# A float32 layer on one core: wide matmuls for the high weight tiles of the up-projection, and another order of the last norm and its stores

## The chip, the core and the metric

The kernel runs on one core of one Trainium2 chip. A core has a matrix engine (TensorE, in the profile PE, with its weight loads as PEld), VectorE (DVE), ScalarE (ACT), GpSimd (POOL) and SyncE (SP), which here mostly issues transfers. Each engine works through its own list of instructions in order and waits on semaphores of the others. TensorE writes its results to PSUM; this kernel's pools there hold eight tiles of up to 512 float32 columns, called banks below. The metric is device time of one execution, in microseconds; a kernel's time is the median of its runs.

## The reference, cut to what matters

One layer of a language model on 256 tokens with a width of 2048, all in float32. Two mixers (a state-space one and a gating one) read one projection of the normed input, are normed, projected back and added to `x`. The change touches only what follows:

```python
h = rmsnorm(x, norm_mlp_g[l])
x = x + jnp.square(jax.nn.relu(h @ w_up[l])) @ w_down[l]     # 2048 -> 8192 -> 2048
...
return rmsnorm(x, norm_final_g)
```

`rmsnorm` multiplies a row by the inverse root of its mean square plus 1e-6 and by a vector of gains.

## The kernel before

**Float32 in three products.** Matmuls here take operands in the format `F32R`. Each float32 operand is kept as two of these: a high part, which is a copy in that format, and a low part, the rest. A product is then three matmuls: high weight by high activation, high weight by low activation, and low weight by high activation. Weights come from memory in float32 and are split on the chip: `wparts` loads two k-steps (2 x 128 rows by 512 columns, 512 KB) into a buffer `raw` (four of them), ScalarE copies it to `whi` (L105), and VectorE subtracts to get `wlo` (L106). There are three buffers each of `whi` and `wlo`, so a split can begin only when TensorE has finished with the buffer three back.

**The two kinds of block.** `block_A` (up-projection, also part of the input projection) holds weights as the stationary operand: for each of four column tiles `m` and each k-step it runs three matmuls of 256 columns, the tokens (L186, L187, L188). Two column tiles share a bank of PSUM, so a block of 512 output features takes two banks. `block_B` (down-projection) holds activations as the stationary operand and streams 512 weight columns (L202 to L204). Both take their banks from one pool of four, `psa`; two other pools, `psx` and `pss`, hold the other four banks for the mixers and the transposes.

**The MLP.** Four rounds `f`, each with four up blocks (16 k-steps, 2048 hidden features in all) and then four down blocks that add to `dacc`. After each up block, for each of its two banks, ScalarE applies ReLU into `rl` (L1004), VectorE multiplies by the positive part, which squares it (L1005, `sqm`), ScalarE copies to the high half of `hT` (L1006) and VectorE subtracts for the low half (L1007). The row factor of the norm before the MLP is applied only at the end, squared, as `rs2q`.

**The end.** The last 512 columns of the last round are done apart: their weights are split ahead into spare memory (`wlast`), then token tile 0 runs with 512 columns and token tile 1 in two halves of 256 (L1048 to L1050, `accL`). `last_add` adds the residual, and squares with a row sum into `ss3` (L984, L987). Then VectorE adds up the row's eight sums (L1054), `rstd_sqrt` makes the inverse root (L268 to L273: a square root on ScalarE, a reciprocal and one Newton step on VectorE), the four quarters of the row tile are scaled (L1059, L1061 on VectorE, L1063 on ScalarE), and each is stored from SyncE's queue (L1064).

**What sets the order.** The order on each engine is not written out: a scheduler places the instructions by its own estimate of when each can run, within what data and buffers allow. It chooses, for example, where the copies of one up block fall between the weight splits of the next.

Of the kernel before, what the change touches and what calls it, by code (L numbers as in the profile page):

```python
# [18 lines left out]
P = 128  # L19
# [30 lines left out]
def hybrid_layer_kernel(  # L50
# [19 lines left out]
    psx = ctx.enter_context(tc.tile_pool(name="psx", bufs=1, space=PSUM))  # L70
    pss_ = ctx.enter_context(tc.tile_pool(name="pss", bufs=3, space=PSUM))
    wp1 = ctx.enter_context(tc.tile_pool(name="wp1", bufs=3))
    tmpool = ctx.enter_context(tc.tile_pool(name="tmpool", bufs=2))
    front = ExitStack()
    sp = front.enter_context(tc.tile_pool(name="ssmp", bufs=1))
# [3 lines left out]
    def nm(s):  # L79
        uid[0] += 1  # L80
        return f"{s}_{uid[0]}"
# [3 lines left out]

    def acc(shape, name="acc"):
        return psa.tile(shape, F32, tag="acc", name=nm(name))
# [103 lines left out]

    def block_B(w, k0, nk, c0, act):

        banks = [acc([P, 512], "accB") for _ in range(2)]
        for kp0, hi, lo in wparts(w, k0, nk, c0):
            for t in range(2):
                ts_ = slice(t * P, t * P + P)
                for kk in range(KS):
                    kp = kp0 + kk
                    xh, xl = act(kp)  # L200
                    with behind():
                        T.matmul(banks[t], xh[:, ts_], hi[:, kk], start=(kp == 0), stop=False)  # L202
                    T.matmul(banks[t], xh[:, ts_], lo[:, kk], start=False, stop=False)  # L203
                    T.matmul(banks[t], xl[:, ts_], hi[:, kk], start=False, stop=(kp == nk - 1))  # L204
                    pump(stream["d"] / 4)
        return banks
# [57 lines left out]
    def rstd_sqrt(dst, ss, scale, n):  # L264

        m = const.tile([P, n], F32, name=nm("rq_m"))
        t1 = const.tile([P, n], F32, name=nm("rq_t"))
        A.activation(dst, ss, AF.Sqrt, scale=scale, bias=eps_c)  # L268
        V.tensor_scalar(m, ss, scale, EPS, ALU.mult, ALU.add)
        V.reciprocal(dst, dst)  # L270
        V.tensor_tensor(t1, dst, dst, ALU.mult)
        V.scalar_tensor_tensor(t1, t1, -0.5, m, ALU.mult, ALU.mult)
        V.scalar_tensor_tensor(dst, t1, 1.5, dst, ALU.add, ALU.mult)  # L273
# [699 lines left out]
    front.close()  # L973
    mp = ctx.enter_context(tc.tile_pool(name="mlp", bufs=1))
# [6 lines left out]
    def last_add(t, c, cw, bank):  # L981
# [6 lines left out]
        if c < D - 512:  # L988
            V.tensor_tensor(d_, d_, gfin[:, c : c + cw], ALU.mult)


    def act_x2T(k):
        return x2T[:, k, 0], x2T[:, k, 1]

    NF = 4
    for f in range(NF):
        hT = []
        for cb in range(4):
            banks = block_A(w_up, 0, 16, f * 2048 + cb * 512, act_x2T)
            ht = mp.tile([P, 4, 2, S], F32R, tag="hT", bufs=6, name=nm("hT"))  # L1000
            for i in range(2):
                rl = mp.tile([P, 2, S], F32, tag="rl", bufs=2, name=nm("rl"))
                sq = mp.tile([P, 2, S], F32, tag="sqm", bufs=2, name=nm("sqm"))
                A.activation(rl, banks[i], AF.Relu)  # L1004
                V.scalar_tensor_tensor(sq, banks[i], 0.0, rl, ALU.max, ALU.mult)  # L1005
# [32 lines left out]
    for t in range(2):  # L1038
        ts_ = slice(t * P, t * P + P)
        cw = 512 if t == 0 else 256  # L1040
        for c in range(0, 512, cw):
            bank = acc([P, cw], "accL")
            for kp0, hi, lo in parts:
                for kk in range(KS):
# [5 lines left out]
                    T.matmul(bank, xl[:, ts_], wh, start=False, stop=(kp == 15))  # L1050
            last_add(t, c0 + c, cw, bank)
        s3 = const.tile([P, 1], F32, name=nm("s3"))
        r3 = const.tile([P, 1], F32, name=nm("r3"))
        V.tensor_reduce(s3, ss3[:, t], AX.X, ALU.add)  # L1054
        rstd_sqrt(r3, s3, 1.0 / D, 1)
        for n in range(4):
            ns = slice(n * 512, (n + 1) * 512)
            if n == 0:
                V.tensor_scalar(dacc[:, t, ns], dacc[:, t, ns], r3, None, ALU.mult)  # L1059
            elif n == 3:  # L1060
                V.scalar_tensor_tensor(dacc[:, t, ns], dacc[:, t, ns], r3, gfin[:, ns], ALU.mult, ALU.mult)  # L1061
            else:
                A.activation(dacc[:, t, ns], dacc[:, t, ns], AF.Copy, scale=r3)  # L1063
            nc.sync.dma_start(out[t * P : (t + 1) * P, ns], dacc[:, t, ns])  # L1064
# [29 lines left out]
```

## Time and profile before

| | |
|---|---|
| three timed runs | 1059.5, 1062.08, 1062.22 us; median 1062.08 |
| the profiled execution: time, span | 1060.78 us, 1059.0 us |
| TensorE busy | 1043.3 us (99%) |
| VectorE, ScalarE busy | 651.3 us (62%), 532.1 us (50%) |
| up blocks' matmuls, first and last start | 331.7 and 962.3 us |
| mean granted clock of TensorE | 0.994 |
| moved by DMA | 195.25 MB, 184 GB/s |

The span runs from the first to the last instruction; the execution's time has 1.78 us around it. A row of the timeline gives start, length in microseconds, engine, line and operation, the tile written and the tiles read, shapes, and in brackets how long the engine had been idle and what ended that. Names of tiles stand without their buffer numbers. The length of a matmul row contains the way through the array, and rows overlap, so the rate of a stream is read from the starts.

### The profile page before, as it was taken

What the parts mean: (1) busy time and instruction counts of PE and PEld (TensorE: products, weight loads), DVE (VectorE), ACT (ScalarE), POOL (GpSimd) and SP (SyncE); (2) the same over time, 40 slices, a digit from 0 to 9 for tenths busy, and PEclk for the clock granted to TensorE, in tenths of its full rate; (3) what the DMA queues carried; (4) which work ended last, traced back from release to release, by engine and by line L of the source; (5) the groups of instructions that cost most, each with busy time, mean ns of one, the idle gap of its engine ahead of it and who ended that gap; (6) DMA issues with size and microseconds to landing.
All of it is one profiled execution on the core that took longest, in us unless ns stands there. A gap on an engine that the chain in (4) does not pass through costs nothing.

```text
span 1059.0 us, 16980 instructions
## 1 busy us (share of the span) xinstructions
PE 1043.3 (99%) x6881; PEld 951.1 (90%) x6881; DVE 651.3 (62%) x888; ACT 532.1 (50%) x685; POOL 9.5 (1%) x22
## 2 busy tenths in 40 slices
PE   8999999999999999999999999999999999999996
PEld 7997899978989999888999988899998889998886
DVE  6899988686687555544455555545555565555564
ACT  5668676663766444544444443344444434444453
POOL 0101000000000000000000000000000000000000
PEclk8999999999999999999999999999999999999998
DMA  8774554566565666666666666666666666666662
GB/s 239 225 224 133 141 159 105 155 219 196 181 221 178 180 183 184 191 193 192 192 181 182 187 189 196 198 182 183 184 187 191 191 197 182 184 184 187 195 205 97
DMA packets 112047, 195.25 MB, mean 184 GB/s; under 512 B 17753, under 2 KB 21537, under 8 KB 111521
## 3 DMA queue, kind: packets, MB, share of 16 engines
q1 hardware_dynamic: 111712, 194.13, 61.4%
q8 instruction: 54, 0.88, 0.4%
q14 instruction: 25, 0.20, 0.1%
q0 software_dynamic: 256, 0.03, 0.0%
HBM read 189.91 MB, written 4.19 MB: 183 GB/s over the span
## 4 chain that ended last, share of the span: by engine, by line
PE 90%; ACT 3%; DVE 3%; DMA 2%; issue 1%; SPq 0%; ACTq 0%
PE accA L186 14%; PE accA L188 14%; PE accA L187 14%; PE accB L203 14%; PE accB L204 14%; PE accB L202 14%; PE pf L664 1%; DMA raw<-in_w_in_dram 1%; ACT Tp L631 1%; DMA bcn<-in_ssm_c_im_dram 1%; DVE wlo L106 1%; PE py L704 1%; PE accL L1050 1%; PE accL L1049 1%; PE accL L1048 1%
## 5 line engine op out<-in xcount | busy, mean ns | idle before, releaser
L106 DVE TENSOR_TENSOR wlo<-raw,whi 128x1024 fp32r<-128x1024 f32 (+1 forms) x337 | 411.3, 1221 | 372.1 <-ACT whi L105 371.5
L105 ACT ACTIVATE whi<-raw 128x1024 fp32r<-128x1024 f32 (+1 forms) x337 | 355.9, 1058 | 454.9 <-PE accB L204 200.9
L186 PE MATMUL accA<-x2T,whi 128*128 128x256 f32 x1024 | 289.6, 283 | 0.0
L187 PE MATMUL accA<-x2T,whi 128*128 128x256 f32 x1024 | 289.6, 283 | 0.0
L188 PE MATMUL accA<-x2T,wlo 128*128 128x256 f32 x1024 | 289.2, 283 | 0.0
L187 PEld LDWEIGHTS accA<-x2T,whi 128*128 128x128 f32 x1024 | 196.6, 192 | 0.2
L186 PEld LDWEIGHTS accA<-x2T,whi 128*128 128x128 f32 x1024 | 196.6, 192 | 0.2
L188 PEld LDWEIGHTS accA<-x2T,wlo 128*128 128x128 f32 x1024 | 196.3, 192 | 0.0
L203 PE MATMUL accB<-wlo,hT 128*128 128x512 f32 x480 | 186.8, 389 | 0.0
L204 PE MATMUL accB<-whi,hT 128*128 128x512 f32 x480 | 186.7, 389 | 0.0
L202 PE MATMUL accB<-whi,hT 128*128 128x512 f32 x480 | 168.0, 389 | 0.0
L204 PEld LDWEIGHTS accB<-whi,hT 128*128 128x128 f32 x480 | 90.1, 188 | 18.7
L203 PEld LDWEIGHTS accB<-wlo,hT 128*128 128x128 f32 x480 | 90.1, 188 | 18.5
L202 PEld LDWEIGHTS accB<-whi,hT 128*128 128x128 f32 x480 | 90.1, 188 | 18.6
L186 PE MATMUL accA<-xT,whi 128*128 128x256 f32 x256 | 73.5, 294 | 2.4 <-ACT xT L300 2.4
L187 PE MATMUL accA<-xT,whi 128*128 128x256 f32 x256 | 73.8, 291 | 0.0
L188 PE MATMUL accA<-xT,wlo 128*128 128x256 f32 x256 | 72.5, 290 | 0.0
L186 PEld LDWEIGHTS accA<-xT,whi 128*128 128x128 f32 x256 | 49.3, 195 | 3.3 <-ACT xT L300 2.7
L187 PEld LDWEIGHTS accA<-xT,whi 128*128 128x128 f32 x256 | 50.0, 195 | 0.6 <-DVE xT L301 0.3
L188 PEld LDWEIGHTS accA<-xT,wlo 128*128 128x128 f32 x256 | 49.5, 196 | 0.2
L203 PE MATMUL accB<-wlo,xT 128*128 128x512 f32 x64 | 25.8, 403 | 0.0
L204 PE MATMUL accB<-whi,xT 128*128 128x512 f32 x64 | 25.1, 392 | 0.0
(285 smaller groups left out, 1079.9 us busy)
## 6 DMA issues: line engine op xcount, KB each, us to landing
raw<-in_w_up_dram SPq DMA_DIRECT2D x128, 512.0 KB, 3.7
raw<-in_w_down_dram SPq DMA_DIRECT2D x128, 512.0 KB, 4.0
raw<-in_w_in_dram SPq DMA_DIRECT2D x47, 512.0 KB, 4.2
raw<-in_w_out_dram SPq DMA_DIRECT2D x32, 512.0 KB, 4.7
raw<-in_ssm_glu_w_dram SPq DMA_DIRECT2D x8, 512.0 KB, 4.4
x<-in_x_dram SPq DMA_DIRECT2D x2, 1024.0 KB
out_dram<-dacc SPq DMA_DIRECT2D x8, 256.0 KB, 2.6
xin<-in_x_dram SPq DMA_DIRECT2D x6, 256.0 KB, 7.1
```

Source lines behind the costliest of these rows:

```text
L105: A.activation(hi, src, AF.Copy)
L106: V.tensor_sub(lo, src, hi.bitcast(F32))
L186: T.matmul(o, hi[:, kk, ms], xh, start=first, stop=False, skip_group_check=True)
L187: T.matmul(o, hi[:, kk, ms], xl, start=False, stop=False, skip_group_check=True)
L188: T.matmul(o, lo[:, kk, ms], xh, start=False, stop=(kp == nk - 1), skip_group_check=True)
L202: T.matmul(banks[t], xh[:, ts_], hi[:, kk], start=(kp == 0), stop=False)
L203: T.matmul(banks[t], xh[:, ts_], lo[:, kk], start=False, stop=False)
L204: T.matmul(banks[t], xl[:, ts_], hi[:, kk], start=False, stop=(kp == nk - 1))
L631: A.activation(Tp[e * 32 : (e + 1) * 32, :, g, 3 - e : 4, :], k4[:, :, 0 : e + 1, :], AF.Copy, scale=gmask[:, g : g + 1],)
L664: T.matmul(pfs[r][i][:, q], w1s[r][:, i, q], u2[r][:, q], start=True, stop=True)
L704: last = T.matmul(py[g * 64 : (g + 1) * 64, q], Gp[:, q, g].rearrange("p j c -> p (j c)"), Eg[:, q, g], start=False, stop=True, skip_group ...
L1048: T.matmul(bank, xh[:, ts_], wh, start=(kp == 0), stop=False)
```

## The change

**Up-projection.** A new `block_A2` takes the place of `block_A` in the MLP. Each column tile `m` gets a bank of its own with two halves. The high weight tile multiplies the high and the low activations in one matmul of 512 columns (they lie side by side in `x2T`), so the first half collects high by high and the second high by low. The low weight tile multiplies the high activations, 256 columns, into the second half. After the block the halves are added: ScalarE copies the second half to a new tile `cr`, VectorE adds the first. ReLU and square then read `cr`. A block needs four banks, so after the mixers are done `psx` and `pss` are given up and their four banks become a second pool, `psm`; `acc` takes four tiles from one pool and four from the other in turn.

**The last norm.** The sums of the row's first seven eighths (of tile 0: three quarters) are added up and scaled ahead of the last `last_add` (L1081, L1082 of the changed kernel), and the square root takes this as its bias with the last sum as its input. The last half's gain is applied ahead for the first 256 columns of tile 1's last quarter. The columns finished last are scaled first and stored first; two pieces go out through ScalarE's queue.

```diff
+    def block_A2(w, k0, nk, c0, act):
+        banks = [acc([P, 2, S], "accA") for _ in range(4)]
+        for kp0, hi, lo in wparts(w, k0, nk, c0):
+            for m in range(4):
+                o = banks[m]
+                ms = slice(m * P, m * P + P)
+                for kk in range(KS):
+                    kp = kp0 + kk
+                    xhl = act(kp)
+                    T.matmul(o, hi[:, kk, ms], xhl, start=(kp == 0), stop=False, skip_group_check=True)
+                    T.matmul(
+                        o[:, 1], lo[:, kk, ms], xhl[:, 0], start=False, stop=(kp == nk - 1),
+                        skip_group_check=True,
+                    )
+        return banks
...
-    def rstd_sqrt(dst, ss, scale, n):
+    def rstd_sqrt(dst, ss, scale, rest, n):
...
-        A.activation(dst, ss, AF.Sqrt, scale=scale, bias=eps_c)
-        V.tensor_scalar(m, ss, scale, EPS, ALU.mult, ALU.add)
+        A.activation(dst, ss, AF.Sqrt, scale=scale, bias=rest)
+        V.tensor_scalar(m, ss, scale, rest, ALU.mult, ALU.add)
...
     front.close()
+    psm = ctx.enter_context(tc.tile_pool(name="psm", bufs=4, space=PSUM))
+    acc_pools[:] = [psa] * 4 + [psm] * 4
...
-            banks = block_A(w_up, 0, 16, f * 2048 + cb * 512, act_x2T)
+            banks = block_A2(w_up, 0, 16, f * 2048 + cb * 512, lambda k: x2T[:, k])
...
-                A.activation(rl, banks[i], AF.Relu)
-                V.scalar_tensor_tensor(sq, banks[i], 0.0, rl, ALU.max, ALU.mult)
+                cr = mp.tile([P, 2, S], F32, tag="cr", bufs=2, name=nm("cr"))
+                for mm in range(2):
+                    b_ = banks[i * 2 + mm]
+                    A.activation(cr[:, mm], b_[:, 1], AF.Copy)
+                    V.tensor_tensor(cr[:, mm], b_[:, 0], cr[:, mm], ALU.add)
+                A.activation(rl, cr, AF.Relu)
+                V.scalar_tensor_tensor(sq, cr, 0.0, rl, ALU.max, ALU.mult)
...
+            if c + cw == 512:
+                s3 = const.tile([P, 1], F32, name=nm("s3"))
+                V.tensor_reduce(s3, ss3[:, t, 0 : (c0 + c) // 256], AX.X, ALU.add)
+                V.tensor_scalar(s3, s3, 1.0 / D, EPS, ALU.mult, ALU.add)
             last_add(t, c0 + c, cw, bank)
...
-        V.tensor_reduce(s3, ss3[:, t], AX.X, ALU.add)
-        rstd_sqrt(r3, s3, 1.0 / D, 1)
+        i3 = (D - cw) // 256
+        rstd_sqrt(r3, ss3[:, t, i3 : i3 + 1], 1.0 / D, s3, 1)
+        o_ = out[t * P : (t + 1) * P]
+        for a, b, eng, q in (
+            (D - cw, D, None, nc.sync), (512, 1024, A, nc.scalar), (0, 512, V, nc.sync),
+            (1024, D - 512, V, nc.sync), (D - 512, D - cw, A, nc.scalar),
+        ):
```

**Where the instructions now stand.** Three places, with the line numbers of each kernel; numbers behind names tell buffers apart.

TensorE, second up block, the same weight buffer, column tiles 0 and 1 (one bank before, two banks now). Before:

```order
L186 MATMUL accA_3969<-x2T,whi_4033 128x256
L187 MATMUL accA_3969<-x2T,whi_4033 128x256
L188 MATMUL accA_3969<-x2T,wlo_4034 128x256
L186 MATMUL accA_3969<-x2T,whi_4033 128x256
L187 MATMUL accA_3969<-x2T,whi_4033 128x256
L188 MATMUL accA_3969<-x2T,wlo_4034 128x256
L186 MATMUL accA_3969<-x2T,whi_4033 128x256
L187 MATMUL accA_3969<-x2T,whi_4033 128x256
L188 MATMUL accA_3969<-x2T,wlo_4034 128x256
L186 MATMUL accA_3969<-x2T,whi_4033 128x256
L187 MATMUL accA_3969<-x2T,whi_4033 128x256
L188 MATMUL accA_3969<-x2T,wlo_4034 128x256
```

Now:

```order
L208 MATMUL accA_3922<-x2T,whi_3972 128x512
L209 MATMUL accA_3922<-x2T,wlo_3973 128x256
L208 MATMUL accA_3922<-x2T,whi_3972 128x512
L209 MATMUL accA_3922<-x2T,wlo_3973 128x256
L208 MATMUL accA_3923<-x2T,whi_3972 128x512
L209 MATMUL accA_3923<-x2T,wlo_3973 128x256
L208 MATMUL accA_3923<-x2T,whi_3972 128x512
L209 MATMUL accA_3923<-x2T,wlo_3973 128x256
```

Twelve matmuls of 256 columns became four of 512 and four of 256; the column tiles still follow each other.

ScalarE, from the end of the first up block into the second (`whi` are splits of the second block's weights, the rest is the first block's result). Before:

```order
L105 ACTIVATE whi_3973<-raw_3971 128x1024
L105 ACTIVATE whi_4003<-raw_4001 128x1024
L1004 ACTIVATE rl_3957<-accA_3714 128x512
L105 ACTIVATE whi_4033<-raw_4031 128x1024
L1004 ACTIVATE rl_3963<-accA_3715 128x512
L1006 ACTIVATE hT_3956<-sqm_3958 128x2x256
L105 ACTIVATE whi_4063<-raw_4061 128x1024
L1006 ACTIVATE hT_3956<-sqm_3964 128x2x256
```

Now:

```order
L109 ACTIVATE whi_3928<-raw_3926 128x1024
L109 ACTIVATE whi_3950<-raw_3948 128x1024
L1029 ACTIVATE cr_3902<-accA_3719 128x256
L1029 ACTIVATE cr_3902<-accA_3720 128x256
L1029 ACTIVATE cr_3913<-accA_3721 128x256
L109 ACTIVATE whi_3972<-raw_3970 128x1024
L1029 ACTIVATE cr_3913<-accA_3722 128x256
L1031 ACTIVATE rl_3900<-cr_3902 128x512
L109 ACTIVATE whi_3994<-raw_3992 128x1024
L1031 ACTIVATE rl_3911<-cr_3913 128x512
L1033 ACTIVATE hT_3899<-sqm_3901 128x2x256
L109 ACTIVATE whi_4016<-raw_4014 128x1024
```

Three copies stand ahead of the third split, the fourth copy and a ReLU ahead of the fourth; `hT` moved behind the fourth split.

ScalarE at the end of the program (`junk` is the square with its row sum, `r` the inverse root). Before:

```order
L1063 ACTIVATE dacc<-dacc,r_1498_10131 128x512 x2
L987 ACTIVATE junk_1502_10199,ss_3712<-dacc 128x256
L987 ACTIVATE junk_1504_10251,ss_3712<-dacc 128x256
L268 ACTIVATE r_1506_10254<-s_1505_10253,eps_c 128x1
L1063 ACTIVATE dacc<-dacc,r_1506_10254 128x512 x2
```

Now:

```order
L1101 DMA out_dram<-dacc 128x512
L1012 ACTIVATE junk_1566_9373,ss_3717<-dacc 128x256
L1012 ACTIVATE junk_1569_9429,ss_3717<-dacc 128x256
L291 ACTIVATE r_1570_9431<-ss_3717,s_1568_9425 128x1
L1100 ACTIVATE dacc<-dacc,r_1570_9431 128x512
L1100 ACTIVATE dacc<-dacc,r_1570_9431 128x256
L1101 DMA out_dram<-dacc 128x512
L1101 DMA out_dram<-dacc 128x256
```

The square root now reads the last sum itself, and ScalarE issues two stores of its own behind its activations.

More of the change, by code (lines that the diff above doesn't have):

```diff
@@ L69, in hybrid_layer_kernel @@
     psa = ctx.enter_context(tc.tile_pool(name="psa", bufs=4, space=PSUM))
-    psx = ctx.enter_context(tc.tile_pool(name="psx", bufs=1, space=PSUM))
-    pss_ = ctx.enter_context(tc.tile_pool(name="pss", bufs=3, space=PSUM))
     wp1 = ctx.enter_context(tc.tile_pool(name="wp1", bufs=3))
@@ L74, in hybrid_layer_kernel @@
     front = ExitStack()
+    psx = front.enter_context(tc.tile_pool(name="psx", bufs=1, space=PSUM))
+    pss_ = front.enter_context(tc.tile_pool(name="pss", bufs=3, space=PSUM))
     sp = front.enter_context(tc.tile_pool(name="ssmp", bufs=1))
@@ L84, in blk @@
         return blkp.tile(shape, dt, tag="blk", name=nm(name))
+    acc_pools = [psa]
     def acc(shape, name="acc"):
-        return psa.tile(shape, F32, tag="acc", name=nm(name))
+        acc_pools.append(acc_pools.pop(0))
+        return acc_pools[-1].tile(shape, F32, tag="acc", name=nm(name))
     def aux(shape, name="aux"):
@@ L987, in last_add @@
         A.activation(junk[:, 0:cw], d_, AF.Square, accum_out=ss3[:, t, i : i + 1])
-        if c < D - 512:
+        if c < D - 512 or c + cw < D:
             V.tensor_tensor(d_, d_, gfin[:, c : c + cw], ALU.mult)
-    def act_x2T(k):
-        return x2T[:, k, 0], x2T[:, k, 1]
     NF = 4
@@ L1050, in hybrid_layer_kernel @@
                     T.matmul(bank, xl[:, ts_], wh, start=False, stop=(kp == 15))
+            if c + cw == 512:
+                s3 = const.tile([P, 1], F32, name=nm("s3"))
+                V.tensor_reduce(s3, ss3[:, t, 0 : (c0 + c) // 256], AX.X, ALU.add)
+                V.tensor_scalar(s3, s3, 1.0 / D, EPS, ALU.mult, ALU.add)
             last_add(t, c0 + c, cw, bank)
-        s3 = const.tile([P, 1], F32, name=nm("s3"))
         r3 = const.tile([P, 1], F32, name=nm("r3"))
-        V.tensor_reduce(s3, ss3[:, t], AX.X, ALU.add)
-        rstd_sqrt(r3, s3, 1.0 / D, 1)
[L1056 to L1061, printed above, removed]
-            else:
-                A.activation(dacc[:, t, ns], dacc[:, t, ns], AF.Copy, scale=r3)
-            nc.sync.dma_start(out[t * P : (t + 1) * P, ns], dacc[:, t, ns])
+        i3 = (D - cw) // 256
[5 more added lines that the diff above has]
+        ):
+            if a == b:
+                continue
+            d_ = dacc[:, t, a:b]
+            if eng is None:
+                V.scalar_tensor_tensor(d_, d_, r3, gfin[:, a:b], ALU.mult, ALU.mult)
+            elif eng is V:
+                V.tensor_scalar(d_, d_, r3, None, ALU.mult)
+            else:
+                A.activation(d_, d_, AF.Copy, scale=r3)
+            q.dma_start(o_[:, a:b], d_)
 _INS = ["x", "norm_mix_g", "w_in", "ssm_a_re", "ssm_a_im", "ssm_b_re", "ssm_b_im", "ssm_c_re",
```

## The prediction

> **What bounds the kernel now.** I read the page's busy shares first, then its chain of waits.
>
> ```profile
> PE 1043.3 (99%) x6881; PEld 951.1 (90%) x6881; DVE 651.3 (62%) x888; ACT 532.1 (50%) x685; POOL 9.5 (1%) x22
> PE 90%; ACT 3%; DVE 3%; DMA 2%; issue 1%; SPq 0%; ACTq 0%
> PE accA L186 14%; PE accA L188 14%; PE accA L187 14%; PE accB L203 14%; PE accB L204 14%; PE accB L202 14%; PE pf L664 1%; DMA raw<-in_w_in_dram 1%; ACT Tp L631 1%; DMA bcn<-in_ssm_c_im_dram 1%; DVE wlo L106 1%; PE py L704 1%; PE accL L1050 1%; PE accL L1049 1%; PE accL L1048 1%
> ```
>
> 90% of the chain is TensorE. TensorE's list of waits has seven rows; the longest and the last are
>
> ```profile
> PE accA L186 <- ACT xT L300: 2.4, 1, 2.4
> PE accB L204 <- DVE hl L874: 0.4, 1, 0.4
> ```
>
> and none of the seven lies in the MLP: the up-projection's matmuls wait for nothing. So what counts is the price of one matmul in an unbroken stream, and whether the other engines stay ahead. A matmul's own "us" includes its pipeline, so the price is the distance between starts. First the timeline of TensorE in the up-projection, then the chain in the last down block, where all matmuls have 512 columns (those two rows are 15 matmuls apart):
>
> ```profile
> 422.58 0.28 PE L186 MATMUL accA<-x2T,whi 128*128 128x256 f32 x1
> 422.70 0.28 PE L187 MATMUL accA<-x2T,whi 128*128 128x256 f32 x1
> 422.82 0.28 PE L188 MATMUL accA<-x2T,wlo 128*128 128x256 f32 x1
> 422.94 0.28 PE L186 MATMUL accA<-x2T,whi 128*128 128x256 f32 x1
> ```
>
> ```profile
> 1035.52 0.23 PE accL L1050
> 1038.92 0.23 PE accL L1050
> ```
>
> 256 columns cost 0.120 us: (422.94 - 422.58)/3. 512 columns cost (1038.92 - 1035.52)/15 = 0.2267 us, not 0.240. Twice the columns cost 0.1067 more, so a matmul pays 0.1067 per 256 columns and 0.0133 once. The windows of the second up block and of the first down block give the clock and the supply:
>
> ```profile
> 354.77:377.81 23.04, 23.04 (x194) 23.04 (x193) 12.23 (x13) 10.66 (x13) 0.00 (x0) 1.00 0.63 181
> 424.70:446.40 21.70, 21.70 (x98) 17.98 (x97) 11.76 (x12) 10.62 (x12) 0.00 (x0) 1.00 0.64 190
> ```
>
> The columns are length, busy PE, PEld, DVE, ACT and POOL, granted clock, DMA share and GB/s. The clock is 1.00 in both, so the two prices compare. An up block is 192 matmuls: 192 x 0.120 = 23.04, as the window says.
>
> **The wide matmul.** Per high weight tile two 256-column matmuls (0.240) become one of 512 (0.2267); the low tile keeps its 0.120. A block has 4 column tiles and 16 k-steps, so 64 such pairs of a high and a low tile; 16 blocks have 1024. A pair costs 0.3467 instead of 0.360: a block 22.19 instead of 23.04, all blocks 1024 x 0.0133 = 13.65 us less, all on the path. The trace shows no stream that alternates 512 and 256 columns. Bounds for the pair: 0.340 if the fixed part goes away entirely (768 columns at 0.2267 per 512), which saves 20.5; 0.360 if mixing costs what the merge saves. I take 0.3467, since both streams have that fixed part, with a weight load per matmul in each.
>
> [...]
>
> **The evacuation.** A result now lies in two halves of a bank. Each bank needs one more ScalarE copy (PSUM to SBUF, 256 columns) and one more VectorE add; ReLU and square then read SBUF. Nearest rows:
>
> ```profile
> L918 ACT ACTIVATE gt<-accA,vecs 128x256 f32<-128x256 f32 x8 | 3.3, 470 | 0.5 <-PE accA L188 0.5
> L504 ACT ACTIVATE Ct<-pc 128x256 f32<-128x256 f32 x4 | 1.2, 385 | 0.0
> L984 DVE SCALAR_TENSOR_TENSOR dacc<-accL,rs2q,dacc 128x256 f32<-128x256 f32 x2 | 1.0, 484 | 6.6 <-PE accL L1050 6.6
> ```
>
> A copy costs 0.39 to 0.47 (I take 0.47), an add 0.48. Four of each per block: ScalarE 10.66 + 1.9 = 12.5 and VectorE 12.23 + 1.9 = 14.2 us of 22.2. Neither becomes the bound. What matters is the block's edge, where these steps queue with the weight splits (L105 on ScalarE, then L106 on VectorE). The two engines there before:
>
> ```profile
> 354.44 0.60 ACT L1004 ACTIVATE rl<-accA 128x512 f32<-128x512 f32 x1 [0.56 <-PE accA L188]
> 355.70 1.06 ACT L105 ACTIVATE whi<-raw 128x1024 fp32r<-128x1024 f32 x1 [0.66 <-PE accA L187]
> 356.66 0.58 ACT L1004 ACTIVATE rl<-accA 128x512 f32<-128x512 f32 x1
> 358.63 1.06 ACT L105 ACTIVATE whi<-raw 128x1024 fp32r<-128x1024 f32 x1 [0.87 <-ACT hT L1006]
> ```
>
> ```profile
> 355.07 0.69 DVE L1005 SCALAR_TENSOR_TENSOR sqm<-accA,rl 128x512 f32<-128x512 f32 x1
> 356.79 1.23 DVE L106 TENSOR_TENSOR wlo<-raw,whi 128x1024 fp32r<-128x1024 f32 x1 [1.02 <-ACT whi L105]
> ```
>
> A split starts when TensorE frees its buffer (355.70) and is done at 356.79 + 1.23 = 358.02, 2.3 us later. Each of the three buffers holds two k-steps, which I call a part: eight pairs, from now on 2.77 us. When one buffer comes free TensorE has two full ones left, 5.55 us: the slack is 3.2 us. In the changed order three copies stand ahead of the first split. Their banks' last matmuls start 2.1, 1.4 and 0.7 us before the block's last, and a row is 0.28 us long, so the third copy runs from some 0.4 us before the edge to the edge: delay about nothing. Ahead of the next split stand the fourth copy and a ReLU: 0.1 + 1.06 + 0.47 + 0.6 = 2.2 us after the edge, and its buffer comes free only at 2.8. So the cover is the wait for buffers, and I cost the evacuation at nothing; a delay of d over 3.2 us would cost 16 x (d - 3.2). The block's last activations come some 7 us after its edge; the down-projection needs them in its seventh part, 6 x 12 x 0.2267 = 16 us after it. A bank is reused two blocks later at the earliest.
>
> **Start of the stage.** The first up block now takes all four old banks, two of them from the last w_out block. TensorE, ScalarE and VectorE there before:
>
> ```profile
> 330.57 0.75 DVE L895 SCALAR_TENSOR_TENSOR x<-accB,rsa,x 128x512 f32<-128x512 f32 x1 [0.60 <-PE accB L204]
> 332.37 0.74 DVE L895 SCALAR_TENSOR_TENSOR x<-accB,rsa,x 128x512 f32<-128x512 f32 x1
> ...
> 335.53 0.82 PE L957 MATMUL ptx<-ident,x 128*128 128x128 f32 x6
> ...
> 338.47 1.06 ACT L105 ACTIVATE whi<-raw 128x1024 fp32r<-128x1024 f32 x1 [0.24 <-PE accA L187]
> ...
> 341.34 1.06 ACT L105 ACTIVATE whi<-raw 128x1024 fp32r<-128x1024 f32 x1
> ```
>
> The third and fourth banks come free with the two adds, by 333.1, and are first written some 2 and 5 us after the stage's start at 331.73: no wait. A table load stood between the two splits shown (the fifth part's and the sixth's). In the new order it stands one part earlier, behind the fourth part's split. That split gets the first part's buffer after 14 pairs, one wide matmul and eight transposes of 0.1: 331.73 + 4.85 + 0.23 + 0.8 = 337.6, 0.8 before the 338.47 shown. So the split behind the load starts near 341.34 - 0.8 = 340.5 and is ready near 342.9. It is due after four parts and the transposes, at 331.73 + 11.1 + 0.8 = 343.6. Nothing is lost, but only by 0.7 us; I take 0, and 1 us as the other end. Weights are wanted every 2.77 us instead of 2.88: 181 GB/s becomes 188, under the 190 of the down stage.
>
> **The tail.** The last rows of the chain, and the stores:
>
> ```profile
> 1051.23 0.19 ACT L987 ACTIVATION_READ_ACCUMULATOR junk<-dacc 128x1 f32 x1
> 1051.45 0.16 DVE L1054 TENSOR_REDUCE s<-ss 128x1 f32<-128x8 f32 x1 [0.64 <-ACT junk L987]
> 1051.65 0.29 ACT L268 ACTIVATE r<-s,eps_c 128x1 f32<-128x1 f32 x1 [0.23 <-DVE s L1054]
> 1052.76 1.33 ACT L1063 ACTIVATE dacc<-dacc,r 128x512 f32<-128x512 f32 x2 [0.81 <-DVE r L273]
> ...
> 1054.67 0.41 SPq L1064 DMA_DIRECT2D out_dram<-dacc  x1
> ```
>
> ```profile
> DMA  0000000000499999999989996200000000000000
> GB/s 0 0 0 0 0 0 0 0 0 0 184 369 358 420 338 399 410 348 338 358 277 400 369 369 225 82 0 0 0 0 0 0 0 0 0 0 0 0 0 0
> ```
>
> The reduction leaves the path: the square root follows the accumulator (1051.42) instead of 1051.65, 0.2 us less. The reduction and the scaling of the sum move under the last 48 matmuls. The first store, now 256 columns, again follows one VectorE step of 0.48 us. The last of four stores was issued at 1054.67. In the new order ScalarE's two come behind its two activations: 0.2 us earlier and with three quarters of the columns these end near 1052.56 + 1.0, so the second issue is near 1054.0, 0.6 us earlier. But the window from 1052 to 1060 (slices of 0.2 us) shows the DMA engines full at some 370 GB/s from 1054.1 to 1056.8: the megabyte, not the issuing, sets the end. So I take 0.2 us for the tail, between 0.6 less and 0.3 more (a first use of ScalarE's queue, which the trace does not show).
>
> **The sum.** The profiled execution took 1060.78 us (span 1059.0). 1060.78 - 13.65 - 0.2 = 1046.9. The median of the three timed runs, 1062.08, lies 1.3 above it; for a median I add half of that: 1047.5.
>
> **The rivals.** (a) The pair is bound by weight loads. PEld fills 23.04 of 23.04 in the up block but 17.98 of 21.70 in the down block; a third of the loads goes, and if loads can run ahead, the columns alone remain: pair 0.340, 20.5 less, 1040. [...] Against it: the same 0.0133 fits the 512-column stream, where loads are not full, and the load for the wide matmul must hide under a narrow one, as now, at 0.120. 0.06. (b) The change does not do what it says: wide after narrow pays the fixed part twice, pair 0.360: 1060.6. Against it stand two changes of width, narrow to wide at the first down block and wide to narrow at the first up block:
>
> ```profile
> 424.62 0.28 PE L188 MATMUL accA<-x2T,wlo 128*128 128x256 f32 x1
> 424.74 0.40 PE L202 MATMUL accB<-whi,hT 128*128 128x512 f32 x1
> ```
>
> ```profile
> 331.50 0.39 PE L204 MATMUL accB<-whi,ahl 128*128 128x512 f32 x1
> 331.73 0.28 PE L186 MATMUL accA<-x2T,whi 128*128 128x256 f32 x1
> ```
>
> The narrow one keeps its 0.12, the wide one its 0.23. 0.07. (c) The evacuation holds up the splits: if all four copies and adds and a ReLU and square run in series ahead of a block's first new split, 4 x 0.95 + 0.60 + 0.69 = 5.1 us, TensorE stalls 1.9 us per block, 30 in all: 1077, slower. It turns into a loss from 3.2 + 13.85/16 = 4.1 us of delay on. For it: both engines take their work strictly in the written order. Against it: the order lets three copies run before the edge. 0.05.
>
> **Chances and range.** Forecast 0.82, (a) 0.06, (b) 0.07, (c) 0.05. About 0.3% (3.2 us) can be told from no change. Faster 0.82 + 0.06 = 0.88, same 0.07, slower 0.05. The timed runs spread over 2.7 us, so 1.4 to either side; with the tail, a lost microsecond at the start and small stalls of 0.1 us per block above, and part of (a) below: 1044.5 to 1051.0.
>
> **What would show it.** Right: pairs of starts 0.347 apart, an up block of 22.2 us, no TensorE wait for `whi` or `wlo` in the MLP, the last matmul near 1036.5, the square root right behind the accumulator, the stores' end some 0.2 us closer to it. Wrong: a pair of 0.340 or 0.360, or a wait of TensorE for a split in the third part of each block.

## The result and the profile after

| | before | the change |
|---|---|---|
| median (runs) | 1061.68 us (1059.5 to 1062.22, 4 runs) | 1051.36 us (1050.4 to 1051.55, 4 runs) |
| ratio, 95% interval | | 0.9905 [0.9888, 0.9922] |
| profiled execution: time, span | 1060.78, 1059.0 us | 1051.24, 1049.5 us |
| first start of an up matmul | 331.73 us | 334.36 us |
| last matmul's start | 1050.02 us | 1041.02 us |
| from there to the end of the span | 8.96 us | 8.49 us |

The change is faster, by 10.3 us where 14.2 was forecast: 0.36 us above the upper end of the range. Split by stage, the two profiled executions differ by 11.63 us in the MLP (718.29 to 706.66), by 0.47 in the tail, and by -2.63 ahead of the MLP, where the code is the same.

The page of the change, its busy shares and the first line of its chain, and the first four rows of TensorE's waits (us in total, times, longest):

```profile
PE 1034.4 (99%) x5857; PEld 896.0 (85%) x5857; DVE 674.1 (64%) x957; ACT 551.6 (53%) x748; POOL 9.5 (1%) x22
PE 94%; ACT 3%; DMA 1%; issue 1%; DVE 0%; SPq 0%; DVEq 0%
```

```profile
PE pc L515 <- DMA bcn<-in_ssm_b_im_dram: 1.7, 1, 1.7
PE accA L190 <- ACT xT L323: 1.5, 1, 1.5
PE accB L225 <- ACT whi L109: 1.2, 1, 1.2
PE pwarm L302 <- DVE eps_c L268: 1.1, 1, 1.1
```

TensorE has lost 1024 matmuls and is still the bound. No row of its waits lies in the MLP (the `whi` row is one wait in the mixers, as before).

The windows of the second, third and fourth up stage (four blocks, 256 pairs each; columns as in the prediction):

```profile
511.21:600.05 88.84, 88.84 (x514) 77.65 (x512) 50.77 (x58) 45.64 (x60) 0.00 (x0) 1.00 0.65 191
687.12:777.50 90.38, 90.38 (x514) 78.41 (x512) 51.83 (x60) 45.14 (x59) 0.00 (x0) 1.00 0.62 187
864.56:953.40 88.84, 88.84 (x513) 77.69 (x512) 53.00 (x62) 45.17 (x59) 0.00 (x0) 1.00 0.63 190
```

Before, each of these took 92.15 or 92.16, the second for example:

```profile
511.81:603.96 92.15, 92.15 (x770) 92.15 (x768) 46.91 (x45) 41.34 (x46) 0.00 (x0) 1.00 0.63 184
```

Two stages of the change have the forecast pair: 88.84/256 = 0.3470 us. The third takes 90.38, or 0.3531, at the same clock of 1.00 and without a wait. The first stage went from 93.01 to 89.78 with its transposes. The four differences, 3.23 + 3.31 + 1.77 + 3.31 = 11.62, are the whole gain of the MLP.

A block's edge on ScalarE and on VectorE (the block before ends at 555.63):

```profile
554.49 0.39 ACT L1029 ACTIVATE cr<-accA 128x256 f32<-128x256 f32 x1 [0.17 <-PE accA L209]
555.18 0.39 ACT L1029 ACTIVATE cr<-accA 128x256 f32<-128x256 f32 x1 [0.31 <-PE accA L209]
555.76 1.06 ACT L109 ACTIVATE whi<-raw 128x1024 fp32r<-128x1024 f32 x1 [0.19 <-PE accA L208]
556.72 0.36 ACT L1029 ACTIVATE cr<-accA 128x256 f32<-128x256 f32 x1
```

```profile
555.22 1.08 DVE L1030 TENSOR_TENSOR cr<-accA,cr 128x256 f32<-128x256 f32 x3
556.85 1.23 DVE L110 TENSOR_TENSOR wlo<-raw,whi 128x1024 fp32r<-128x1024 f32 x1 [0.55 <-ACT whi L109]
```

The split waits for TensorE to free its buffer (555.76), not for the copies; the third copy is done by then. Its low half is ready at 558.08, and due two parts of 2.78 us after the edge, 561.2: 3.1 us of slack.

The tail, from the row sum to the two queues' stores:

```profile
1042.18 0.19 ACT L1012 ACTIVATION_READ_ACCUMULATOR junk<-dacc 128x1 f32 x1
1042.40 0.29 ACT L291 ACTIVATE r<-ss,s 128x1 f32<-128x1 f32 x1
...
1044.02 1.30 SPq L1101 DMA_DIRECT2D out_dram<-dacc  x3
1044.26 0.84 ACTq L1101 DMA_DIRECT2D out_dram<-dacc  x2
```

The square root follows the accumulator's reading (1042.37) by 0.03 us, with no reduction between. The first store is issued 3.00 us after the last matmul's start (1041.02), and the last issue ends 4.30 after it. Before, with the last matmul's start at 1050.02, these were 3.25 and 5.05:

```profile
1053.27 1.80 SPq L1064 DMA_DIRECT2D out_dram<-dacc  x4
```

Ahead of the MLP, windows from 5 to 35 and from 27 to 35 us, of before and then of the change, and the change's longest wait there:

```profile
5.00:35.00 30.00, 26.81 (x189) 25.01 (x189) 19.38 (x64) 18.52 (x38) 0.00 (x0) 0.89 0.93 250
27.00:35.00 8.00, 8.00 (x64) 7.53 (x64) 4.62 (x22) 5.62 (x12) 0.00 (x0) 1.00 0.97 211
```

```profile
5.00:35.00 30.00, 26.51 (x163) 24.25 (x163) 18.45 (x59) 16.81 (x34) 0.00 (x0) 0.89 0.91 247
27.00:35.00 8.00, 7.69 (x39) 6.92 (x40) 5.55 (x24) 3.86 (x9) 0.00 (x0) 0.57 0.87 195
```

```profile
27.31 0.89 PE L515 MATMUL pc<-ident,bcn 64*128 64x64 f32 x6 [1.68 <-DMA bcn<-in_ssm_b_im_dram]
```

Between 27 and 35 us TensorE ran 64 matmuls before and 39 in the change. The trace's record of the granted clock has a stretch at half clock (a granted clock of 0.5) from 27.80 to 34.63 in the change, behind the 1.68 us wait for a load, and none there in before. Earlier on the two kernels are alike. Before's record has half clock from 8.64 to 15.46. The change's record begins only at 14.15, but until then its 256-column matmuls start 0.213 us apart, and 0.120 afterwards:

```profile
12.14 0.41 PE L192 MATMUL accA<-xT,wlo 128*128 128x256 f32 x1
12.35 0.41 PE L190 MATMUL accA<-xT,whi 128*128 128x256 f32 x1
12.56 0.41 PE L191 MATMUL accA<-xT,whi 128*128 128x256 f32 x1
```

Up to the first up matmul TensorE runs the same matmuls in the same order in both kernels, so their starts can be matched one by one. The change is 0.94 us ahead at 24 us, 0.66 behind after the wait for the load, 2.95 behind at 36 and, as before itself loses 0.3 near 78, 2.64 behind at the first up matmul. So 1.6 us came from that wait and 2.3 from the half clock behind it. Whether this comes from the change is asked below.

### The profile page after: what moved, and what is told of

It reads as the page before. It is cut to its first block, busy times and chain, and to the rows that moved or that the text cites. A ratio compares the mean times of both kernels' runs of the same rounds, so it can differ in the third digit from the quotient of the medians.

```text
span 1049.5 us, 15062 instructions
## 1 busy us (share of the span) xinstructions
PE 1034.4 (99%) x5857; PEld 896.0 (85%) x5857; DVE 674.1 (64%) x957; ACT 551.6 (53%) x748; POOL 9.5 (1%) x22
## 4 chain that ended last, share of the span: by engine, by line
PE 94%; ACT 3%; DMA 1%; issue 1%; DVE 0%; SPq 0%; DVEq 0%
PE accA L208 23%; PE accB L226 14%; PE accB L227 14%; PE accB L225 14%; PE accA L209 11%; PE accA L190 4%; PE accA L191 4%; PE accA L192 4%; PE pf L687 1%; ACT Tp L654 1%; PE py L727 1%; ACT whi L109 1%; DMA bcn<-in_ssm_b_im_dram 1%; PE accL L1077 1%; PE accL L1075 1%; PE accL L1076 1%
## 5 line engine op out<-in xcount | busy, mean ns | idle before, releaser
L208 PE MATMUL accA<-x2T,whi 128*128 128x512 f32 x1024 | 355.4, 395 | 0.0
L209 PE MATMUL accA<-x2T,wlo 128*128 128x256 f32 x1024 | 280.3, 278 | 0.0
L208 PEld LDWEIGHTS accA<-x2T,whi 128*128 128x128 f32 x1024 | 191.6, 188 | 43.7
L209 PEld LDWEIGHTS accA<-x2T,wlo 128*128 128x128 f32 x1024 | 192.6, 188 | 1.8
L1029 ACT ACTIVATE cr<-accA 128x256 f32<-128x256 f32 x64 | 24.0, 374 | 7.9 <-PE accA L209 7.9
L227 PE MATMUL accB<-whi,xT 128*128 128x512 f32 x64 | 25.1, 392 | 0.0
L225 PE MATMUL accB<-whi,xT 128*128 128x512 f32 x64 | 23.9, 401 | 1.2 <-ACT whi L109 1.2
```

The costliest lines, as they stand in the source:

```text
L208: T.matmul(o, hi[:, kk, ms], xhl, start=(kp == 0), stop=False, skip_group_check=True)
L209: T.matmul(o[:, 1], lo[:, kk, ms], xhl[:, 0], start=False, stop=(kp == nk - 1), skip_group_check=True,)
L1029: A.activation(cr[:, mm], b_[:, 1], AF.Copy)
```

## The experiments

The runs are called e1 to e14; those told together are not always neighbours in number.

Theories on the two parts of the gap. For the pair: W (changes of width cost), B (the narrow matmul adds into a bank just written), C (a fixed price of the wide matmul), and, after the first four runs, L against P. For the part ahead of the MLP: scatter (S) or the new queue.

### The two halves of the change alone

The up-projection alone keeps `block_A2` and takes back the tail; the tail alone takes `block_A` and its evacuation back. Of the second edit, the first line (all edits below stand in part):

```diff
-            banks = block_A2(w_up, 0, 16, f * 2048 + cb * 512, lambda k: x2T[:, k])
+            banks = block_A(w_up, 0, 16, f * 2048 + cb * 512, lambda k: (x2T[:, k, 0], x2T[:, k, 1]))
```

Run e1:

> The up-projection of the change with the tail of before (no sums ahead, no second queue). In the profile of the change the MLP was 11.6 us shorter than before, the tail 0.5 shorter and the part ahead of the MLP 2.6 longer. Theory 1 (the pair carries nearly all, the front's 2.6 us is scatter from execution to execution): 1061.7 - 11.6 = 1050.1 to 1051.5 for the median, some 0.5 us above or on the change itself; pairs 0.3488 apart; the first up matmul anywhere between 331 and 335 us. Rival (the second queue shifts the front): the first up matmul near 331.7, as before, and the median under the change's, near 1049.5.

Measured: 1048.65 us (1047.99 to 1051.13, 5 runs) against 1061.09 of before (17 runs), ratio 0.9877 [0.9858, 0.9896]; below the 1050.1 to 1051.5 expected. MLP 706.66, stages 88.84, 90.38 and 88.84 again, tail 8.85. First up matmul at 333.82, without the second queue.

Run e2:

> The tail of the change with the up-projection of before (three 256-column matmuls per pair). Theory 1: only the tail's 0.5 us or less: 1061.0 to 1061.7; last matmul to the end of the span 8.5 us instead of 9.0; the first up matmul anywhere between 331 and 335. Rival (the second queue shifts the front): the first up matmul near 334.4 as in the change, and the median some 2 us above before, near 1063.5.

Measured: 1061.06 us (1059.74 to 1063.97, 12 runs), ratio 0.9996 [0.9983, 1.0008]. Tail 8.65 instead of 8.96; first up matmul at 331.07, with the second queue.

What follows: the up-projection carries the gain; the tail's third to half a microsecond is below what these runs can tell. The start of the MLP was late without the second queue and early with it, so the queue isn't its cause. And the 17 runs of before lie in two groups, nine from 1059.88 to 1061.09 and eight from 1062.26 to 1064.31; the up-projection alone has three from 1047.99 to 1048.65 and two at 1050.73 and 1051.13. In e1 itself a gap of some 2.5 us between the groups' means thus opens in both kernels. In the other rounds the times of before spread as far, but some lie between the groups (1061.50, 1061.54, 1061.77).

### Fewer changes of width, and another bank

```diff
-                for kk in range(KS):
-                    T.matmul(o, hi[:, kk, ms], ...)
-                    T.matmul(o[:, 1], lo[:, kk, ms], ...)
+                for kk in range(KS):
+                    T.matmul(o, hi[:, kk, ms], ...)
+                for kk in range(KS):
+                    T.matmul(o[:, 1], lo[:, kk, ms], ...)
```

Run e3:

> The two k-steps of a column tile in the order wide, wide, narrow, narrow: half as many changes of width, the same banks. Theory W (the 2.1 ns that a pair takes over 0.3467 come with the changes of width): half of it goes, pairs 0.3478 on average, the MLP 1.1 us shorter (705.6), the median near 1050.3. Theory B (they come from the narrow matmul adding into the half bank that the wide one ahead of it has just written): one narrow in two still follows a wide one into its bank, and the other adds into what was written one matmul earlier; also a half or nothing, 705.6 to 706.7. Theory C (a fixed price of the wide matmul with two operand rows, whatever stands beside it): no change, 706.7.

Measured: 1047.51 us (1046.73 to 1050.52, 5 runs), ratio 0.9871 [0.9853, 0.9890]; MLP 706.32. All three later stages take 89.15 to 89.16:

```profile
510.30:599.46 89.16, 89.16 (x513) 77.84 (x512) 50.93 (x58) 45.65 (x61) 0.00 (x0) 1.00 0.62 190
```

For the other bank, column tiles run inside the k-steps and the narrow matmul of a tile comes one wide matmul later:

```diff
+            todo = [(m, kk) for kk in range(KS) for m in range(4)]
+            for s in range(len(todo) + 1):
+                # wide matmul of todo[s], then the narrow one of todo[s - 1]
```

Run e4:

> Wide and narrow still alternate, but the narrow matmul belongs to the column tile before, so that it adds into another bank than the wide one ahead of it. Theory W (changes of width): pair stays 0.3488, the MLP 706.7, no change. Theory B (same bank just written): pair 0.3467, the MLP 2.1 us shorter, 704.6, the median near 1049.3. Theory C: no change.

Measured: 1054.21 us (1051.23 to 1055.38, 6 runs), ratio 0.9920 [0.9902, 0.9938]; MLP 710.20:

```profile
511.97:602.10 90.13, 90.13 (x514) 78.45 (x513) 50.98 (x57) 44.80 (x60) 0.00 (x0) 1.00 0.63 188
```

What follows: none of the three theories accounts for the pair. Half the changes of width saved 0.34 us, not the 1.1 of W; and there a wide matmul with a wide one behind it took 0.233 us and a narrow one with a narrow one behind it 0.115 (means over 527 and 529 starts), where uniform streams have 0.2267 and 0.120. Another bank was slower by 3.5 us, where B wanted 2.1 less; but e4 moved other matmuls too, so its 0.352 us per pair can't be put down to the bank alone. What B and C can't explain lies in the change itself: the same wide and narrow matmuls, adding into one bank, take 0.3467 in two of its stages and 0.353 in another. The stages, not the pairs, are the clue. In the change the pair's mean is 0.350 in the first three parts, then 0.3467 to the end of stages two and four, and 0.353 to the end of stage three.

### The order at a stage's entry

The program's orders (W wide, N narrow) of the first three parts of a stage differ in one place only, the third part:

```
stages 2 and 4:  WWWWNWNNWNNWNNWN WWNWNNWNWNWNWNWN WWWWNWNNWNNWNNWN WNWNWNWN...
stage 3:         WWWWNWNNWNNWNNWN WWNWNNWNWNWNWNWN WWNWNNWNWNWNWNWN WNWNWNWN...
```

So theory L: the order at the entry sets a beat (a pattern of distances between starts that repeats) which the alternation then keeps; its rival P is that something else about the third stage, its buffers or its moment, does it. In the change's second stage four pairs take 520.66 - 519.27 = 1.39 us:

```profile
519.27 0.40 PE L208 MATMUL accA<-x2T,whi 128*128 128x512 f32 x1
...
520.66 0.40 PE L208 MATMUL accA<-x2T,whi 128*128 128x512 f32 x1
```

In its third stage the beat is three pairs long and takes 700.83 - 699.77 = 1.06 us (0.35, 0.35, 0.36):

```profile
699.77 0.40 PE L208 MATMUL accA<-x2T,whi 128*128 128x512 f32 x1
700.00 0.28 PE L209 MATMUL accA<-x2T,wlo 128*128 128x256 f32 x1
700.12 0.40 PE L208 MATMUL accA<-x2T,whi 128*128 128x512 f32 x1
700.35 0.28 PE L209 MATMUL accA<-x2T,wlo 128*128 128x256 f32 x1
700.47 0.40 PE L208 MATMUL accA<-x2T,whi 128*128 128x512 f32 x1
700.71 0.28 PE L209 MATMUL accA<-x2T,wlo 128*128 128x256 f32 x1
700.83 0.40 PE L208 MATMUL accA<-x2T,whi 128*128 128x512 f32 x1
```

The change once more, its third stage with the order of the others, and the reverse (there each matmul of the part is tied behind the one before it):

```diff
+            if third and kp0 == 2 * KS:
+                todo = third
...
-            banks = block_A2(..., lambda k: x2T[:, k])
+            banks = block_A2(..., lambda k: x2T[:, k], wide4 if f == 2 and cb == 0 else None)
# the reverse:       wide2 if f in (1, 3) and cb == 0 else None
```

Run e5:

> The change itself once more, beside runs of before on this chip. Theory S (the part ahead of the MLP scatters from execution to execution, with before and with the change alike): the times fall into two groups some 2.7 us apart, as those of before (about 1060.4 and 1063.4) and of the two other variants did; the lower group near 1048.3, the upper near 1051.1, the median in either; gain within one group 12.1 us. Rival (the second queue of the change holds the front up): all times near 1051.3, the first up matmul at 334.3 or later. The third up stage again 90.38 us, the second and fourth 88.84, if their length is set by the program.

Measured: 1048.53 us (1046.93, 1047.78, 1049.29, 1049.89) against 1061.50 of before (7 runs), ratio 0.9882 [0.9862, 0.9903]. Stages 88.84, 90.38, 88.84; first up matmul at 332.99. The same program that gave 1051.36 gave 1048.53 here; the rival wanted 1051.3 in all.

Run e6:

> In the change the second and fourth up stages took 88.84 us (347.0 ns per pair), the third 90.38 (353.1). Their instructions stand in the same order but for the third part of weights: four wide matmuls first in stages two and four, two wide first in stage three. Here stage three gets the order of the other two. Theory L (the order at the stage's entry sets a beat that the alternation then keeps): stage three 88.84 us too, the MLP 705.1, the times 1.5 us below those of the change in each group. Rival P (something else about the third stage, such as its buffers or its moment): stage three stays at 90.38.

Measured: stage three

```profile
686.51:775.35 88.84, 88.84 (x513) 77.70 (x512) 51.79 (x60) 45.17 (x59) 0.00 (x0) 1.00 0.61 190
```

and the MLP 705.12. The median is 1049.22 (1049.10 to 1049.64, 4 runs), not below that of the change beside it: the profiled run has a wait for the same load and half clock from 27.18 to 34.01, and the mean granted clock of the four runs is 0.991 to 0.994, against 0.994 to 0.996 in e5.

Run e7:

> The reverse: the third part of stages two and four gets the order that stage three has, two wide matmuls first. Theory L: all three stages take 90.38 us, the MLP 709.7, one time 3 us above the change's, about 1051.3 to 1054.3. Rival P: stages two and four stay at 88.84, stage three at 90.38.

Measured: 1055.1 us in one run, above the 1051.3 to 1054.3 expected; the first up matmul at 335.13, later than in any other profile, with half clock from 78.67 to 85.50; the stages

```profile
511.97:602.35 90.38, 90.38 (x513) 78.47 (x512) 50.84 (x58) 45.63 (x60) 0.00 (x0) 1.00 0.62 187
689.42:779.80 90.38, 90.38 (x513) 78.41 (x512) 51.84 (x60) 45.13 (x59) 0.00 (x0) 1.00 0.59 187
866.87:957.25 90.38, 90.38 (x514) 78.49 (x512) 53.08 (x62) 45.15 (x59) 0.00 (x0) 1.00 0.60 187
```

What follows: L is shown both ways, to a hundredth of a microsecond. Sixteen matmuls in another order set the length of the 232 pairs behind them, 346.7 or 353.3 ns. Of the 6.6 ns between the two, 4.5 are the wide matmul's (its start to the next start, 231.5 and 236.0 ns) and 2.1 the narrow one's (115.2 and 117.3). What in the array keeps the beat isn't shown.

A third order, with one change of width per eight matmuls:

```diff
+            for m in range(4):        # eight wide ones, then
+            for m in range(4):        # eight narrow ones
```

Run e10:

> In each part all eight wide matmuls stand first and then the eight narrow ones: one change of width per eight matmuls. Theory W (each change of width costs): pair near 346.7 + 2/8 = 346.9, every stage 88.8. Theory L (a repeated order keeps one beat through a stage, whatever the number of changes; two of the orders tried kept 347.0, 353.1, one 348.3): all stages equal to 0.1 us, at one value between 88.8 and 90.4.

Measured: 1047.76 us in one run, three stages of 89.36 (0.3491 per pair).

```profile
507.62:596.98 89.36, 89.36 (x513) 78.65 (x512) 50.43 (x56) 44.70 (x58) 0.00 (x0) 1.00 0.61 189
```

Fewer changes of width are not the better order: 2 per 16 matmuls cost more than 16 per 16 do in the good beat, 89.36 us per stage against 88.84.

### Four times the evacuation

```diff
-                    A.activation(cr[:, mm], b_[:, 1], AF.Copy)
-                    V.tensor_tensor(cr[:, mm], b_[:, 0], cr[:, mm], ALU.add)
+                    for _ in range(4):
+                        A.activation(cr[:, mm], b_[:, 1], AF.Copy)
+                        V.tensor_tensor(cr[:, mm], b_[:, 0], cr[:, mm], ALU.add)
```

Run e9:

> Each copy and add of the evacuation done four times over (the repeats compute the same values). Written order on ScalarE: three copies ahead of a block's first new split, then four ahead of each of the next three. A copy waits for the add before it, about 0.85 us for both. Theory E (the cover is the slack of the weight buffers, 3.2 us in the forecast, 3.1 in the change's profile: split begun 555.76, its low half done 558.08, due 561.2): second split 1.8 us late, third 3.5, fourth 5.2, so TensorE stalls some 2 us per block, 16 blocks: 1048.5 + 32, about 1080. Rival F (the evacuation lies beside everything and never reaches the splits): stages 88.84, 90.38, 88.84 as in the change, time 1047 to 1052.

Measured: 1051.1 us in one run, stages 88.84, 90.38, 88.84: nothing lost. ScalarE at the same edge:

```profile
555.62 1.06 ACT L109 ACTIVATE whi<-raw 128x1024 fp32r<-128x1024 f32 x1
556.59 1.19 ACT L1030 ACTIVATE cr<-accA 128x256 f32<-128x256 f32 x4
558.45 1.06 ACT L109 ACTIVATE whi<-raw 128x1024 fp32r<-128x1024 f32 x1 [0.67 <-ACT cr L1030]
```

The expectation went wrong on the price: the scheduler took the four banks in turn, so a copy didn't wait for its own add, and a round of four copies took 1.19 us, not 3.4. That fits between two splits 2.8 us apart, of which a split takes 1.06. So the slack was not used up, and how far it reaches was not tried; that the evacuation costs nothing stands, and there was room for three times as much again.

### The part ahead of the MLP

Eight more warm-up matmuls behind the transposes of the first two pieces of `x`:

```diff
+        if i == 1:
+            with tc.issue_after(tr.ins):
+                for _ in range(8):
+                    T.matmul(pwarm, onesm, onesm, start=True, stop=True)
```

Run e8:

> The change with eight more warm-up matmuls behind the first eight transposes, where TensorE stood idle from 7.3 to 9.7 us (before) and from 7.6 to 9.1 (the change). Theory S1 (an idle stretch there costs 6.8 us at half clock, from 8.6 to 15.5 in before): no half clock between 8.6 and 15.5, the matmuls there 0.12 apart, TensorE 2.5 us ahead at 15. Then it comes to the transposes that want the load landing at 27.3 about 2.5 us early and idles there for 2 to 4 us; if idling sets the half clock, it falls on 27.8 to 34.6 in every run, the times are in one group, and the start of the MLP is no earlier: 333.5 to 334.5, times 1050.5 to 1051.5. Rival S2 (the half clock comes at its own moments whatever TensorE does): a half-clock stretch between 5 and 16 us as before, two groups of times.

Measured: 1047.90 us (1046.9 to 1048.19, 4 runs), ratio 0.9875 [0.9854, 0.9895]; first up matmul at 331.03.

```profile
27.00:35.00 8.00, 8.00 (x55) 7.75 (x56) 5.39 (x20) 4.76 (x10) 0.00 (x0) 0.79 1.08 323
```

```profile
PE accA L192 <- DVE wlo L110: 0.5, 1, 0.5
...
PE pc L522 <- DMA bcn<-in_ssm_b_im_dram: 0.2, 1, 0.2
```

The first half of S1 held: no half clock from 3.99 to 27.89, and 256-column matmuls 0.120 us apart at 10 us. The second didn't: TensorE lost part of its lead in waits for weights (0.5 and less) and came to the late load only 0.2 us early. There still was half clock from 27.89, for 3.41 us instead of 6.83. The times are one group, as S1 said, but the low one, where S1 expected 1050.5 to 1051.5.

Then both edits together, and with the transposes of `bcn` tied behind a later matmul:

```diff
+                    with tc.issue_after(done[44].ins):
                         T.transpose(pc[:, h8]..., (bn if which == 0 else cn)[:, h2 * 8 + h8], ident[rs_, rs_])
```

Run e11:

> The change with both edits: the eight more warm-ups behind the first transposes, and the third up stage in the order of the other two. If the two are independent: the one group of times of the filled front (1046.9 to 1048.2) less 1.54: 1045.4 to 1046.7, median 1046.4; all stages 88.84. Rival (the gain of one is taken back by the other's half-clock stretch): 1047.9 or above.

Measured: 1045.78 us (1045.09 to 1046.72, 4 runs), ratio 0.9865 [0.9848, 0.9881]; MLP 705.12, all stages 88.84. Against e8 that is 2.1 us, where the stage's profile has 1.54; the two ran on different chips, and e11's profile has no half clock ahead of the tail.

Run e12:

> As the one before, and the transposes that wait for the load landing at 27.3 us stand some 57 matmuls later in TensorE's order, so that it has work when it gets there. Theory S1 (idling brings the half clock): no half clock after 27, 1.7 us earlier at the MLP's start than with the filled front alone (331.0), 329.3, median 1044.7. Rival (what these transposes feed is then late further on, since they are 6.8 us later): TensorE waits for it, start of the MLP 331 or later, median 1046.4 or above.

Measured: 1044.43 us (1044.13 to 1044.83, 4 runs), ratio 0.9849 [0.9834, 0.9864]; first up matmul at 329.07. From 5 to 35 us:

```profile
5.00:35.00 30.00, 28.90 (x226) 26.61 (x226) 20.81 (x68) 18.74 (x37) 0.00 (x0) 1.00 0.95 285
```

226 matmuls, eight of them the added ones, where before had 189 and the change 163, and no half clock recorded until the end of the program. This version beats both kernels: 15.8 us under before.

Last, the same quiet front put into before and into the change with its own orders:

Run e13:

> Before, with the eight more warm-ups and the later transposes and nothing of the change. Theory S1 (idling brings the half clock, in before as in the change): no half clock ahead of the MLP, the first up matmul near 329.1, the times in one group less than 1 us wide, near 1057.6 (329.1 + the 718.3 of before's MLP + 9.0 + 1.8 outside the span = 1058.2, or 0.6 less where the profiled runs lie above the others). Rival: two groups as before, 1060.4 and 1063.4, or all later than before.

Measured: 1059.08 us (1057.97 to 1059.64, 11 runs), ratio 0.9981 [0.9971, 0.9992]; the spread of 1.7 us is above the 1 us expected, and the median above 1058.2. First up matmul at 329.21, no half clock recorded ahead of the tail. The 15 runs of before beside it spread from 1059.01 to 1063.86.

```profile
5.00:35.00 30.00, 28.01 (x219) 25.79 (x219) 21.30 (x72) 18.81 (x37) 0.00 (x0) 1.00 0.97 287
```

Run e14:

> The change with the same quiet front and its own orders of the up stages. From the last run: 1044.43 + 1.54 (the third stage's beat) = 1046.0, in one group. Against the kernel of e13 the change then gains 11.6 (the MLP) + 0.5 (the tail) = 12.1 us, not 13.85: what is missing is the third stage's 1.54 and the stages' starts. Rival (the scatter made up all of the miss): a difference of 13.5 or more.

Measured: 1046.68 us (1046.08 to 1047.16, 4 runs), ratio to before 0.9868 [0.9852, 0.9883]; first up matmul at 329.99; stages 88.84, 90.38, 88.84. Against e13 the change gains 1059.08 - 1046.68 = 12.4 us.

What follows: both kernels scatter ahead of the MLP, and with the idle stretches filled the spread shrinks from 4.9 us to 1.7 in before, and in the change from 4.6 (its eight runs in the result and in e5) to 1.1. With this quiet front the change gains 12.4 us, not 10.3 and not 14.2; its stages and tail alone give 12.1.

The profiles show what makes the times differ. All eleven without the added matmuls still run at half clock at 12 us, on record or by the 0.213 us spacing, and until 13.5 to 15.7 us; in the five with them the spacing there is 0.120. A second, late stretch, near 28 or near 79 us, stands in eight of the eleven: there the first up matmul starts at 332.99 to 335.13, in the other three at 330.29 to 331.73. So early and late executions are, in the profiles, those without and with the late stretch. The mean granted clock says the same of the 46 runs of before beside the experiments: 13 runs at 0.995 or more took 1059.01 to 1061.77 us, 12 runs at 0.993 or less 1062.05 to 1064.31, and the 21 at 0.994 lie across both.

One thing stays open. The late stretch is in eight of the nine unfilled profiles with the new up-projection and in neither of the two with the old one. The runs' clocks show that before falls into it too, but not that it does so as often.

## Why the prediction missed, step by step

**What bounds the kernel: right.** TensorE's stream set the time, and the gain came out of the distance between starts. The 13.3 ns fixed part holds: two stages ran at 88.84 against 256 x 0.34667 = 88.75.

**"A pair costs 0.3467 instead of 0.360", 13.65 us: the term that was mis-sized.** The pair has this price in the two stages with the good beat and not over the whole: the MLP gained 11.63. Of the missing 2.0, the third stage has 1.6 (90.38 - 88.75), which e6 took away and e7 tripled; the other 0.4 lies mostly in the stages' first parts, where wide and narrow ones stand in another order and a pair takes 0.350. The prediction said that no stream of before alternates 512 and 256 columns, and took two single changes of width as evidence against a mixing cost. Two changes that stand alone could not show a beat of three pairs (1.06 us in stage three). The bounds, 0.340 to 0.360, held.

**The median and its spread: the step that failed outright.** "The timed runs spread over 2.7 us, so 1.4 to either side" treats the scatter as noise about one value, and about 0.6 us were added for it. No term of the sum stood for the part ahead of the MLP, where the code is the same. But the late half clock and the wait in front of it took 3.9 us in the change's profile and are absent in others, so a median of four can fall on either side: 1051.36 the first time, 1048.53 in e5. Against 12.4 with a quiet front, the first comparison lost 2.1 us to this. So of the 3.9 us between 14.2 and 10.3 about half is the beat and half the scatter. Either alone would have stayed within the range; that they fell together and missed its end by only 0.36 us is chance.

**The evacuation at nothing: right**, slack 3.1 for 3.2, and four times as much cost nothing either. The copy took 0.37 (0.47 taken), the add 0.42 (0.48).

**Start of the stage at nothing: right.** The first stage gained 3.23 of the 3.41 that its pairs could give, and none of the rows of waits is the split behind the table load.

**The tail, 0.2: right in kind, small.** 0.47 in the profile, 0.3 in e2's. The first store came 0.25 us closer to the last matmul, as the reduction's place on the path said; the rest is behind the issue, where the first use of ScalarE's queue was feared and cost nothing that shows: its two issues end at 1045.10, ahead of the 1045.32 of SyncE's three.

**The rivals.** (a) fell: no order gave a pair under 0.3467. (c) fell with e9. (b), a price for mixing the widths, was taken for all or nothing, 13.3 ns per pair in every stage; one of the four up stages paid half of it, 6.6 ns behind its entry. The place that (b) named, the wide matmul behind a narrow one, has two thirds of it, the narrow matmul the rest.

## What to carry to other kernels

One stream of unlike matmuls had two steady rhythms here, 0.3467 and 0.3533 us per pair, and 16 matmuls near its entry chose one for the 232 pairs behind them: look at the length of each repeated stage, not at their mean, and where equal stages differ, compare their entry orders. Before forecasting to a third of a per cent, find out what makes the runs of before differ; here eight idle-time matmuls and a later place for a few transposes took 1.05 us off before (e13) and two thirds off its spread. A cost taken as hidden is best tried by multiplying it.

## What was not expected of the hardware

The beat: alternating 512 and 256 columns ran at 0.3467 or at 0.3533 us per pair for 80 us on end, with the same kinds of matmul at a granted clock of 1.00, set by the order of 16 matmuls near the entry. Two wide, two narrow gave 0.3483; eight and eight 0.3491; alternating with another bank 0.3521.

The half clock: recorded stretches of 3.41 and 6.83 us, one of them 6.83 us long 0.5 us behind a wait of 1.68, in executions of one and the same program at different places (27.80 in the change's first profile, 7.48 and 79.16 in its second). With the idle time filled and the transposes later, none is recorded ahead of the tail (e12, e13); with the idle time filled alone, one of 3.41 us was left in e8 and none in e11. The longest single wait at the start of a stretch was 2.45 us (before, where it ends at 9.73 and the half clock begins at 8.64). A wait is not enough: those of 1.2 us between 90 and 97 us, in twelve of the profiles (1.22 us in before, up to 92.78, and in the change, up to 95.42), have no half clock behind them. A wait of 1.0 us at 25.7 was followed by none in e14 and one of 0.97 at 25.5 by 6.83 us in e1. What else decides it, no run here shows; it stays open.
